# Four pieces of the modulation to a burst, in seven buffers, with half of the descriptor scratch, in a one-core hybrid decoder layer

## The chip, the cores and the metric

The kernel runs on one core of a Trainium2 chip. The metric is the device time of one execution in microseconds (us), lower is better. The kernel before took 2662.56 us (median of three runs, 2650.79 to 2666.44). Engines: PE is TensorE (matmul; PEld its weight loads), DVE VectorE, ACT ScalarE, POOL GpSimd, SP SyncE, which here issues most of the DMAs.

## The reference

One layer of a hybrid decoder on 512 prompt tokens (width 2048) and 8 sample tokens. A condition vector c gives six modulation vectors (shift, scale and gate, each for the mixer and for the FFN). One projection feeds two mixers; their outputs are concatenated, projected and added:

```python
ada = silu(c) @ w_ada + b_ada            # 2048 -> 6 * 2048
h = modulate(rmsnorm(x, g_norm_mix), shift1, scale1)
p = h @ w_in                              # 2048 -> 4896 columns
att = banded_attention(q, k, v, ...)      # window 128, ALiBi, sinks, 16 heads on 4
y, S, _ = rwkv7_mix(p[:, 1536:], ...)     # 16 heads of 64, state S (64 x 64) per head
x = x + gate1 * (concat(att, y) @ w_out)
h = modulate(rmsnorm(x, g_norm_ffn), shift2, scale2)
x = x + gate2 * (swiglu(h @ w_ffn_in) @ w_ffn_out)
y = rmsnorm(x, g_norm_final)
```

(The names of this sketch are shortened.) The RWKV-7 mixer is a recurrence over tokens, `S_t = S_{t-1} diag(w_t) + (S_{t-1} a_t) b_t^T + v_t k_t^T`. The kernel computes it in blocks of 32 tokens. Each sample token has its own old state, which is loaded, updated once and stored.

## The kernel before, in words

**Main stream.** Columns are held in two halves of 260 (256 prompt tokens and 4 sample tokens each). Every weight tile is split into a high and a low part, `wh` (ACT, L88) and `wl` (DVE, L91), of a raw tile that SP loads (L86); `mm3` (L98) makes three products of each, so one k step of a main tile is six matmuls of 260 columns. `main_tile` runs 16 k steps into a PSUM tile named `pm`. The in-projection is 39 such tiles; the out-projection's tiles are named `po` and are run in two parts of 8 k steps; `wout_part` begins the first part only when eight tiles of the concatenated heads have been loaded back from DRAM (`catl`, written earlier to `catd` by the RWKV pairs). Then comes the FFN, with sums of weight blocks in a Strassen-like scheme, some of them accumulated by POOL's DMAs.

**Side work.** Everything else is a set of generators in `self.bg`: the second part of the modulation (`ada_gen`), the RWKV pairs (8 pairs of heads: `pG` begins a pair's block matrices; a triangular solve of 31 steps on DVE, `stmp` and `Tt`, turns them into `TT`; `pu`; then the pair's recurrence over blocks, the "chain", with two small `psc` matmuls a step, ACT and DVE copying the state `Z` between them; `pY` and `pg` end the pair), the sample step (four rounds on one buffer `sS`, 512 KB loaded and stored in each), the reloading of the heads (`catl`), decode for the sample tokens and the prompt's attention (`pl` logits, `Lg`, `pt`, `pO`).

**What sets the order.** The engines run their instructions in the order in which the program issues them, so the order is fixed when the kernel is built. After each k step, `main_tile` calls `pump`, which moves a planner's clock of TensorE, `now()`, by 0.62 us and resumes each generator whose due time, `job[1]`, has come; the generator issues instructions until its next `yield`. `spent(eng, us, more)` moves an engine's planned time, and `done_at`, from which the job's next due time is taken. Work issued through `self.px` is charged so; there a `dma_start` is charged 1.0 us and 1.5 more. Since `spent` begins from the later of the engine's planned time and `done_at`, a charge to the tensor engine behind such a load moves the shared clock by the load's 2.5 us too. These are numbers of the planner, not times of the chip.

**The part around the change.** `ada_gen` makes 16 groups of 512 output columns, each from 16 pieces of weights [128 x 512] (256 KB); a piece is loaded into a tile of tag `ar` (3 buffers) and multiplied in four matmuls of 128 columns against the condition vectors, four column groups of the array. Other users of the tag are `ada_finish`, `startup`, the in-projection's spilled tiles (`sp`) and one FFN operand (`s3`). The kernel is built with the default scratch for DMA descriptors of the software queue.

Of the kernel before, what the change touches and what calls it, by code (L numbers as in the profile page):

```python
# [7 lines left out]
F32 = mybir.dt.float32  # L8
# [6 lines left out]
P = 128  # L15
KD = 16
# [47 lines left out]
class Kern:  # L64
# [190 lines left out]

    def ada_finish(self, f0, n, ps):
        nc = self.px
        res = self.w.tile([P, 512], F32, tag="ar", bufs=3, name=self.nm("adar"))
        nc.scalar.copy(res[:, :n * 128], ps[:, :n * 128])
        yield  # L260
        p2 = self.aux("adT")
        for f in range(n):
            nc.tensor.matmul(p2[:, f * 16:f * 16 + 9], res[:, f * 128:(f + 1) * 128], self.sel, start=True, stop=True)
        nc.vector.tensor_tensor(
            self.mod[:, f0:f0 + n, :],
            p2[:, :n * 16].rearrange("p (f t) -> p f t", f=n)[:, :, :9],
            self.par[:, P_BA + f0:P_BA + f0 + n].unsqueeze(2).broadcast_to([P, n, 9]),
            ALU.add,
        )
# [34 lines left out]
    def ada_gen(self):  # L304
        nc = self.px
        for c in (GT1, SH2, SC2, GT2):
            for q in range(4):
                ci = c // 4 + q
                ps = self.hold("ada")
                for k in range(KD):  # L310
                    raw = self.w.tile([P, 512], F32, tag="ar", bufs=3, name=self.nm("ar"))
                    nc.sync.dma_start(raw, self.I["w_ada2"][ci - 8, k])
                    for j in range(4):
                        self.nc.tensor.matmul(
                            ps[32 * j:32 * j + 32, 0:128], self.cT[:, k, :], raw[:, j * 128:(j + 1) * 128],
                            start=k == 0, stop=k == KD - 1, tile_position=(0, 32 * j), skip_group_check=True,
                        )
                    self.spent(self.nc.tensor, 0.3)
                    yield
                    yield  # L320
                res = self.w.tile([P, 512], F32, tag="ar", bufs=3, name=self.nm("adar"))[:, 0:128]
                nc.scalar.copy(res, ps[:, 0:128])
                yield
                p2 = self.aux("adT")
                nc.tensor.transpose(p2[:, 0:128], res, self.ident)
                nc.vector.tensor_tensor(
                    self.mod[:, 4 * ci:4 * ci + 4, :], p2[:, 0:128].rearrange("p (f t) -> p f t", f=4)[:, :, 0:9],
                    self.par[:, P_BA + 4 * ci:P_BA + 4 * ci + 4].unsqueeze(2).broadcast_to([P, 4, 9]), ALU.add)
# [41 lines left out]
    def startup(self):  # L370
        nc, I = self.nc, self.I
        xs = self.x_tiles()
        c = self.w.tile([P, 512], F32, tag="ar", bufs=3, name=self.nm("cr"))[:, 0:144]
        nc.sync.dma_start(c, I["c"].rearrange("p k t -> p (k t)"))
        k = 0
        for t, n in xs:
            nc.sync.dma_start(t, I["x"][:, k:k + n])
            k += n
        xk = [t[:, i] for t, n in xs for i in range(n)]
        nc.vector.memset(self.cT[:, :, 9:32], 0.0)  # L380
        nc.scalar.activation(self.cT[:, :, 0:9], c.rearrange("p (k t) -> p k t", t=9), AF.Silu)
        nc.scalar.activation(c[:, 0:2], self.cT[:, 0, 0:2], AF.Square)
        nc.scalar.activation(c[:, 2:4], c[:, 0:2], AF.Sqrt)
        ps = self.ps_m.tile([P, 2, 512], F32, tag="m", name="ssq1")
        for k in range(0, KD, 2):
            sq = [self.t520(t) for t in (("tC", "tD"), ("tA", "tB"))[k // 2 % 2]]
            nc.scalar.activation(sq[0], xk[k], AF.Square)
            if k % 4:
                nc.vector.tensor_tensor(sq[1], xk[k + 1], xk[k + 1], ALU.mult)
            else:  # L390
                nc.scalar.activation(sq[1], xk[k + 1], AF.Square)
            nc.vector.tensor_tensor(sq[0], sq[0], sq[1], ALU.add)
            for h in range(2):
                nc.tensor.matmul(ps[:, h, :HB], self.ones, sq[0][:, h], start=k == 0, stop=k == KD - 2)
        rstd = self.rstd_of(self.t520("tF"), ps)
        self.pcs, self.ring, self.used = {}, [], set()
        head = []
        for idx in (I_WA, I_G0, I_G1, 8, 0):
            src, m = self.w_in_src(idx)
            head.append((src, m, self.new_pc(idx)[:m, 1:513], self.SC[:m, idx]))  # L400
        self.hk = 0
        self.start(self.seq(self.h_parts(xk, rstd), self.ada_gen()))
        for k0, k1 in ((0, 2), (2, 4), (4, 8), (8, 12), (12, 14), (14, 16)):
            while self.hk < k1:
                self.pump()
            for tile_ in head:
                self.part_tile(*tile_, k0, k1)
# [44 lines left out]
    def filler(self):  # L452

        if not self.spills:
            self.pump()
            return
        idx, dram, scols = self.spills.pop(0)
        nc = self.nc
        ps = self.main_tile(self.I["w_in"][idx], self.hH, self.hL)
        t = self.w.tile([P, 512], F32, tag="ar", bufs=3, name=self.nm("sp"))  # L460
        nc.scalar.copy(t.rearrange("p (h t) -> p h t", h=2), ps[:, :, 0:256])
        nc.vector.tensor_copy(scols, ps[:, :, 256:260])
        nc.sync.dma_start(dram, t)
# [936 lines left out]
    def ffn_in(self, st):  # L1400
# [3 lines left out]
        tc, nc, I = self.tc, self.nc, self.I  # L1404
# [9 lines left out]
        sp = self.fpb.enter_context(tc.tile_pool(name="strw", bufs=1))  # L1414
# [43 lines left out]
        for ht in range(early):  # L1458
            ps = mt("pm")
# [13 lines left out]
        for i, ht in enumerate(order):  # L1473
# [7 lines left out]
            for g in range(2):  # L1481
                a11, a21 = load(ht, 0, 0, g), load(ht, 1, 0, g, places[(2 * i + g) % 4])
                a22 = load(ht, 1, 1, g, "raw")
                a12 = load(ht, 0, 1, g)
                s3 = self.w.tile([P, 512], F32, tag="ar", bufs=3, name=self.nm("s3"))
                nc.gpsimd.dma_start(a21, src(ht, 1, 1, g), accum_op=ALU.add)
                if not (old and g):
                    nc.sync.dma_start(s3, src(ht, 0, 0, g))
                    nc.gpsimd.dma_start(s3, src(ht, 1, 0, g), accum_op=ALU.add)
                if i == 0 and g == 1:  # L1490
                    for _ in norm:
                        pass
                if not old:
                    for col, a, b in ((0, a11, B11), (1, a12, B21)):
                        product(p12[:, col], weights(a), b, g)
                        if i == g == 0:
                            next(norm, None)
                            next(norm, None)
                    if g == 1:
                        first_sums(pc, p12)  # L1500
                nc.vector.tensor_tensor(a11, a21, a11, ALU.add)
                for ps, a, b in ((p45[:, 1], a21, T1), (p67[:, 0], a11, T2), (p67[:, 1], s3, T3),
                                 (p45[:, 0], a22, T4), (p3[:, 0], a12, B22)):
                    product(ps, weights(a), b, g)
                    if b is T1:
                        if old and g:
                            nc.vector.tensor_tensor(s3, a11, a22, ALU.subtract)
                        nc.vector.tensor_tensor(a12, a12, a11, ALU.add)
                        next(rest, None)
                    if i == g == 0:  # L1510
                        next(norm, None)
                        next(norm, None)
                    if g == 0:
                        continue
                    if b is T2:
                        nc.vector.tensor_tensor(pc[:, 1], p67[:, 0, :HB], pc[:, 1], ALU.subtract)  # L1516
                    elif b is T3:
                        cu = ct("cu", 2)
                        nc.vector.tensor_tensor(cu[:, 1], pc[:, 1], p67[:, 1, :HB], ALU.subtract)
                    elif b is T4:  # L1520
                        nc.vector.tensor_tensor(cu[:, 0], cu[:, 1], p45[:, 0, :HB], ALU.subtract)
                        nc.vector.tensor_tensor(pc[:, 1], p45[:, 1, :HB], pc[:, 1], ALU.add)
                        nc.vector.tensor_tensor(cu[:, 1], p45[:, 1, :HB], cu[:, 1], ALU.add)
# [217 lines left out]
```

## Time and profile before

| | us |
|---|---|
| Runs (three), median | 2662.56 (2650.79 to 2666.44) |
| Profiled execution, its own time | 2657.76 |
| Its span | 2656.0 |
| PE busy in the span | 2554.5 (96%) |
| DVE busy | 1723.8 (65%) |
| ACT busy | 1105.9 (42%) |
| POOL busy | 382.5 (14%) |
| Last matmul of the in-projection's main tiles issued at | 926.5 |
| First matmul of the out-projection at | 926.7 |
| Last matmul of the out-projection at | 1207.5 |

Busy time of PE is that of matmuls from start to modelled end; matmuls overlap, so the sum is larger than the time that they hold the array. Times of the trace are from the span's start. In rows of the trace, `x2` behind a matmul counts the records that are put together in the row; one matmul instruction of the FP32 modulation has two records. In the rows of the order below, `x4` counts instructions that are alike.

### The profile page before, as it was taken

Reading aid. Unit: us, or ns where it says so; the run is one execution under the profiler, and the core shown is the slowest. Engines: PE = TensorE matmul, PEld = TensorE weight load, DVE = VectorE, ACT = ScalarE, POOL = GpSimd, SP = SyncE. Lnnn points to the kernel's source line nnn. Section 1 sums busy time; section 2 is a strip of 40 time slices with the busy share of each in tenths; the row PEclk is TensorE's granted clock in tenths of the full one; section 3 lists DMA queues with packets and bytes.
Section 4 is the critical chain, followed back from the end, with each engine's and each line's share of the span. In section 5 each row is a group of like instructions: output and inputs, shape, how many; then the busy total and the mean of one; then the engine's idle time right before and its main releaser. Section 6 shows DMA issues by size and latency. Waiting matters only on the chain. (4 is left out here: it accounts for less than half of the span.)

```text
span 2656.0 us, 59166 instructions
## 1 busy us (share of the span) xinstructions
PE 2554.5 (96%) x23373; PEld 2340.7 (88%) x23373; DVE 1723.8 (65%) x3880; ACT 1105.9 (42%) x2153; POOL 382.5 (14%) x525
## 2 busy tenths in 40 slices
PE   7899999999999999998999999999999999999997
PEld 4677777888787889898999999999999999999997
DVE  5466767777657444678777777777777763444456
ACT  3133444545533324547544444444444532222225
POOL 0012112112112000021111212111121100000004
PEclk9999999999989999999999999999999999999999
DMA  9855445455546675245777777777777552333333
GB/s 347 294 165 154 152 126 162 149 166 160 159 153 207 203 251 146 94 160 183 191 201 204 193 208 198 191 207 198 194 208 200 155 184 92 124 125 102 116 105 106
DMA packets 241704, 460.22 MB, mean 173 GB/s; under 512 B 32353, under 2 KB 44561, under 8 KB 241393
## 3 DMA queue, kind: packets, MB, share of 16 engines
q1 hardware_dynamic: 206880, 379.88, 44.5%
q0 software_dynamic: 33904, 75.50, 13.4%
q8 instruction: 183, 3.00, 0.5%
q10 hardware_dynamic: 640, 1.05, 0.2%
q14 instruction: 97, 0.79, 0.1%
HBM read 421.73 MB, written 35.59 MB: 172 GB/s over the span
## 5 line engine op out<-in xcount | busy, mean ns | idle before, releaser
L88 ACT CAST wh<-raw 128x512 fp32r<-128x512 f32 (+2 forms) x410 | 246.9, 606 | 510.5 <-PE pf L98 278.9
L98 PE MATMUL pf<-go,wh 128*128 128x260 f32 x2560 | 414.1, 281 | 0.0
L91 DVE TENSOR_TENSOR wl<-raw,wh 128x512 fp32r<-128x512 f32 (+2 forms) x410 | 283.8, 694 | 200.4 <-ACT wh L88 194.8
L98 PEld LDWEIGHTS pf<-go,wh 128*128 128x128 f32 x2560 | 354.0, 188 | 0.1
L98 PE MATMUL pm<-hH,wh 128*128 128x260 f32 (+1 forms) x1248 | 301.3, 319 | 7.3 <-ACT wh L88 6.7
L1269 ACT CAST wh<-sr 128x512 fp32r<-128x512 f32 x320 | 198.1, 621 | 261.7 <-PE pm L1439 232.0
L1270 DVE TENSOR_TENSOR wl<-sr,wh 128x512 fp32r<-128x512 f32 x320 | 220.6, 690 | 83.0 <-ACT wh L1269 75.9
L98 PE MATMUL pm<-hH,wl 128*128 128x260 f32 (+1 forms) x1248 | 265.4, 292 | 5.2 <-DVE wl L91 5.1
L98 PE MATMUL pf<-go,wl 128*128 128x260 f32 x1280 | 267.7, 282 | 0.0
L1439 PE MATMUL pm<-xT,wh 128*128 128x260 f32 x1408 | 263.2, 286 | 4.4 <-DVE pc L1516 4.3
L98 PE MATMUL pm<-hL,wh 128*128 128x260 f32 (+1 forms) x1248 | 263.4, 291 | 0.0
L1439 PE MATMUL pm<-T,wh 128*128 128x260 f32 x1408 | 257.6, 283 | 0.0
L98 PEld LDWEIGHTS pm<-hH,wh 128*128 128x128 f32 (+1 forms) x1248 | 196.5, 191 | 57.8 <-issue 31.6
L1439 PEld LDWEIGHTS pm<-xT,wh 128*128 128x128 f32 x1408 | 216.9, 188 | 11.0 <-DVE pc L1516 6.1
L1439 PEld LDWEIGHTS pm<-T,wh 128*128 128x128 f32 x1408 | 216.9, 188 | 0.0
L98 PEld LDWEIGHTS pm<-hH,wl 128*128 128x128 f32 (+1 forms) x1248 | 197.4, 192 | 16.0 <-DVE wl L91 8.7
L1439 PE MATMUL pm<-B0H,wl 128*128 128x260 f32 x704 | 201.4, 286 | 9.6 <-DVE wl L1270 9.1
L98 PEld LDWEIGHTS pm<-hL,wh 128*128 128x128 f32 (+1 forms) x1248 | 196.9, 191 | 7.5 <-issue 5.2
L1439 PE MATMUL pm<-B0H,wh 128*128 128x260 f32 x704 | 200.3, 285 | 2.0 <-DVE acct L1206 1.7
L98 PEld LDWEIGHTS pf<-go,wl 128*128 128x128 f32 x1280 | 200.9, 188 | 0.0
L1439 PE MATMUL pm<-B0L,wh 128*128 128x260 f32 x704 | 198.9, 282 | 0.0
L1439 PE MATMUL pm<-T,wl 128*128 128x260 f32 x704 | 198.7, 282 | 0.0
(427 smaller groups left out, 5243.8 us busy)
## 6 DMA issues: line engine op xcount, KB each, us to landing
ar<-in_w_ada SPq DMA_DIRECT2D x256, 256.0 KB, 3.1
sr<-in_w_fi SPq DMA_DIRECT2D x176, 256.0 KB, 4.6
raw<-in_w_fo SPq DMA_DIRECT2D x176, 256.0 KB, 2.6
raw<-in_w_in SPq DMA_DIRECT2D x144, 256.0 KB, 3.7
araw<-in_w_ada SPq DMA_DIRECT2D x64, 512.0 KB, 6.5
raw<-in_w_fi SPq DMA_DIRECT2D x120, 256.0 KB, 4.6
s<-in_w_fi SPq DMA_DIRECT2D x80, 256.0 KB, 4.4
s<-in_w_fi POOLq DMA_DIRECT2D x80, 256.0 KB, 5.1
```

Source lines behind the costliest of these rows:

```text
L88: nc.scalar.copy(wh[:, :n], raw[:, :n])
L91: nc.vector.tensor_tensor(wl[:, :n], raw[:, :n], wh[:, :n].bitcast(F32), ALU.subtract)
L98: nc.tensor.matmul(ps[:m, bank, :HB], w, a[:, k, h, :], start=first and i == 0, stop=last and i == 2, skip_group_check=True,)
L1269: nc.scalar.copy(H, src)
L1270: nc.vector.tensor_tensor(L, src, H.bitcast(F32), ALU.subtract)
L1439: nc.tensor.matmul(ps[:, :HB], x[:, s], y, start=g == k == i == 0, stop=g == 1 and k == 3 and i == 2, skip_group_check=True)
```

## The change

The loop over 16 pieces becomes a loop over four bursts of four. A burst takes four tiles of tag `ar`, issues their four loads directly on SP (`self.nc.sync`, so that the planner isn't charged), moves its own due time by 2.5 us, yields, issues the 16 matmuls, charges the tensor engine 0.8 us, and yields twice. All users of the tag now name seven buffers. The scratch for the software queue's descriptors is set to 8192 bytes a partition, half of the default; the four more buffers take 8192 bytes a partition.

```diff
-                for k in range(KD):
-                    raw = self.w.tile([P, 512], F32, tag="ar", bufs=3, name=self.nm("ar"))
-                    nc.sync.dma_start(raw, self.I["w_ada2"][ci - 8, k])
-                    for j in range(4):
-                        self.nc.tensor.matmul(
-                            ps[32 * j:32 * j + 32, 0:128], self.cT[:, k, :], raw[:, j * 128:(j + 1) * 128],
-                            start=k == 0, stop=k == KD - 1, tile_position=(0, 32 * j), skip_group_check=True,
-                        )
-                    self.spent(self.nc.tensor, 0.3)
+                for k0 in range(0, KD, 4):
+                    raws = [self.w.tile([P, 512], F32, tag="ar", bufs=7, name=self.nm("ar")) for _ in range(4)]
+                    for k, raw in enumerate(raws, k0):
+                        self.nc.sync.dma_start(raw, self.I["w_ada2"][ci - 8, k])
+                    self.done_at += 2.5
+                    yield
+                    for k, raw in enumerate(raws, k0):
+                        for j in range(4):
+                            self.nc.tensor.matmul(
+                                ps[32 * j:32 * j + 32, 0:128], self.cT[:, k, :], raw[:, j * 128:(j + 1) * 128],
+                                start=k == 0, stop=k == KD - 1, tile_position=(0, 32 * j), skip_group_check=True,
+                            )
+                    self.spent(self.nc.tensor, 0.8)
                     yield
                     yield
...
-    nc = bacc.Bacc("TRN2", target_bir_lowering=False, num_devices=1)
+    nc = bacc.Bacc("TRN2", target_bir_lowering=False, num_devices=1, dynamic_dma_scratch_size=8192)
```

The other lines of the diff only put `bufs=7` where the tag had `bufs=3`.

How the order of the instructions changes. On TensorE, within the in-projection, a stretch with two visits to the modulation (`ada`), before:

```order
L314 MATMUL ada_7262<-ar_7469,cT 32x128 x4
L49 MATMUL psc<-Z_1732,L_803_5453 32x64 x2
L49 MATMUL pT_7482<-cst,KB_6829 128x128 x4
L98 MATMUL pm_7231<-hH,wh_7491 128x260 x2
L98 MATMUL pm_7231<-hL,wh_7491 128x260 x2
L98 MATMUL pm_7231<-hH,wl_7492 128x260 x2
L49 MATMUL psc<-Z_1732,LS_1736 64x64 x2
L98 MATMUL pm_7231<-hH,wh_7491 128x260 x2
L98 MATMUL pm_7231<-hL,wh_7491 128x260 x2
L98 MATMUL pm_7231<-hH,wl_7492 128x260 x2
L314 MATMUL ada_7262<-ar_7514,cT 32x128 x4
```

and a burst of the kernel after:

```order
L98 MATMUL pm_4010<-hH,wl_4070 128x260 x2
L49 MATMUL psc<-Z_1738,L_288_1790 32x64 x2
L98 MATMUL pm_4010<-hH,wh_4069 128x260 x2
L98 MATMUL pm_4010<-hL,wh_4069 128x260 x2
L98 MATMUL pm_4010<-hH,wl_4070 128x260 x2
L318 MATMUL ada_4052<-ar_4053,cT 32x128 x4
L318 MATMUL ada_4052<-ar_4054,cT 32x128 x4
L318 MATMUL ada_4052<-ar_4055,cT 32x128 x4
L318 MATMUL ada_4052<-ar_4056,cT 32x128 x4
L49 MATMUL psc<-Z_1738,LS_1742 64x64 x2
L98 MATMUL pm_4010<-hH,wh_4069 128x260 x2
```

The pieces stood alone between main matmuls and chain steps (`psc`); now four stand in a row. All 256 pieces stood in 261 runs of rows; they now stand in 76. The first `pG` of pairs 0 to 7 stood behind 630, 870, 1218, 1530, 1824, 2154, 2454 and 2760 of the 3744 instructions of `pm` tiles; it now stands behind 780, 1176, 1542, 2010, 2448, 2868, 3390 and 3744 (six instructions to a pump).

On TensorE, at the seam of the two projections, before:

```order
L98 MATMUL pm_11547<-hH,wh_11648 128x260 x2
L98 MATMUL pm_11547<-hL,wh_11648 128x260 x2
L98 MATMUL pm_11547<-hH,wl_11649 128x260 x2
L98 MATMUL po_11721<-cH_11377,wh_11724 128x260 x2
L98 MATMUL po_11721<-cL_11378,wh_11724 128x260 x2
L98 MATMUL po_11721<-cH_11377,wl_11725 128x260 x2
L98 MATMUL po_11721<-cH_11377,wh_11724 128x260 x2
```

and after, from the last `pm` row on:

```order
L98 MATMUL pm_10557<-hH,wl_10678 128x260 x2
L49 MATMUL pT_10753<-cst,tA_10444 128x128 x4
L49 MATMUL pG_10767<-KB_10734,tA_10444 32x64 x9
L49 MATMUL psc<-Z_1739,L_1159_7956 32x64 x2
L49 MATMUL pG_10767<-KB_10734,tA_10444 32x64 x7
L49 MATMUL pG_10768<-KB_10734,tA_10444 32x64 x5
L49 MATMUL psc<-Z_1739,LS_1744 64x64 x2
L49 MATMUL pG_10768<-KB_10734,tA_10444 32x64 x11
L49 MATMUL pu_10810<-TT,L_1350_9422 128x128 x3
L49 MATMUL psc<-Z_1739,L_1159_7956 32x64 x2
L49 MATMUL pu_10810<-TT,L_1350_9422 128x128
L49 MATMUL pY_10822<-Z_1739,RR_9140 32x64 x17
```

Behind the last `pm` row, 231 rows without a main matmul follow before the first `po` row. They hold pair 7 from `pT` and `pG` on, the end of chain 5 and chains 6 and 7, the sample step, decode, and the attention of the first two pairs of heads with part of the next.

On DVE, where the first round of the sample step (`sS`, `stt`, `sa`) stands, before:

```order
L49 TENSOR_TENSOR stt_10164<-sS_10162,X_9975 128x1024
L49 TENSOR_REDUCE L_1083_7530<-pY_10291 128x8
L49 TENSOR_REDUCE sa<-stt_10164 128x16
L49 TENSOR_SCALAR L_1083_7530<-L_1083_7530 128x8
L49 COPY Z_1733<-psc 32x64
L49 TENSOR_TENSOR stt_10164<-sa,X_9975 128x1024
L49 TENSOR_TENSOR RR_8293<-pY_10291,L_1083_7530 128x512
L49 TENSOR_TENSOR sS_10162<-sS_10162,stt_10164 128x1024
L49 TENSOR_REDUCE L_1083_7530<-RR_8293 128x8
L49 TENSOR_SCALAR Z_1733<-psc,PC_8538 64x64
L91 TENSOR_TENSOR wl_10528<-raw_10525,wh_10527 128x512
L49 TENSOR_TENSOR sS_10162<-sS_10162,stt_10164 128x1024
```

and after:

```order
L49 COPY Z_1739<-psc 32x64
L49 TENSOR_REDUCE L_1350_9422<-RR_10199 128x8
L49 TENSOR_TENSOR stt_11280<-sS_11278,X_11169 128x1024
L49 TENSOR_SCALAR Z_1739<-psc,PC_10352 64x64
L49 TENSOR_REDUCE sa<-stt_11280 128x16
L49 RECIPROCAL L_1350_9422<-L_1350_9422 128x8
L49 TENSOR_TENSOR stt_11280<-sa,X_11169 128x1024
L49 TENSOR_TENSOR RR_10199<-RR_10199,L_1350_9422 128x512
L49 TENSOR_TENSOR sS_11278<-sS_11278,stt_11280 128x1024
L49 COPY Z_1739<-psc 32x64
L49 TENSOR_SCALAR Z_1739<-psc,PC_10352 64x64
L49 TENSOR_TENSOR sS_11278<-sS_11278,stt_11280 128x1024
```

Before, the round stood between the splits `wl` of the in-projection's weights; now it stands between the copies `Z` of a chain, with no split near it. On SP the eight `catl` loads stood among the raw loads of the in- and out-projection; they now stand behind FFN weight loads (`sq`, `rstd`, `acc`) that take over buffers of decode.

More of the change, by code (lines that the diff above doesn't have):

```diff
@@ L257, in ada_finish @@
         nc = self.px
-        res = self.w.tile([P, 512], F32, tag="ar", bufs=3, name=self.nm("adar"))
+        res = self.w.tile([P, 512], F32, tag="ar", bufs=7, name=self.nm("adar"))
         nc.scalar.copy(res[:, :n * 128], ps[:, :n * 128])
@@ L309, in ada_gen @@
                 ps = self.hold("ada")
-                for k in range(KD):
-                    raw = self.w.tile([P, 512], F32, tag="ar", bufs=3, name=self.nm("ar"))
-                    nc.sync.dma_start(raw, self.I["w_ada2"][ci - 8, k])
-                    for j in range(4):
-                        self.nc.tensor.matmul(
-                            ps[32 * j:32 * j + 32, 0:128], self.cT[:, k, :], raw[:, j * 128:(j + 1) * 128],
-                            start=k == 0, stop=k == KD - 1, tile_position=(0, 32 * j), skip_group_check=True,
-                        )
-                    self.spent(self.nc.tensor, 0.3)
+                for k0 in range(0, KD, 4):
[11 more added lines that the diff above has]
+                    self.spent(self.nc.tensor, 0.8)
                     yield
                     yield
-                res = self.w.tile([P, 512], F32, tag="ar", bufs=3, name=self.nm("adar"))[:, 0:128]
+                res = self.w.tile([P, 512], F32, tag="ar", bufs=7, name=self.nm("adar"))[:, 0:128]
                 nc.scalar.copy(res, ps[:, 0:128])
@@ L372, in startup @@
         xs = self.x_tiles()
-        c = self.w.tile([P, 512], F32, tag="ar", bufs=3, name=self.nm("cr"))[:, 0:144]
+        c = self.w.tile([P, 512], F32, tag="ar", bufs=7, name=self.nm("cr"))[:, 0:144]
         nc.sync.dma_start(c, I["c"].rearrange("p k t -> p (k t)"))
@@ L459, in filler @@
         ps = self.main_tile(self.I["w_in"][idx], self.hH, self.hL)
-        t = self.w.tile([P, 512], F32, tag="ar", bufs=3, name=self.nm("sp"))
+        t = self.w.tile([P, 512], F32, tag="ar", bufs=7, name=self.nm("sp"))
         nc.scalar.copy(t.rearrange("p (h t) -> p h t", h=2), ps[:, :, 0:256])
@@ L1484, in ffn_in @@
                 a12 = load(ht, 0, 1, g)
-                s3 = self.w.tile([P, 512], F32, tag="ar", bufs=3, name=self.nm("s3"))
+                s3 = self.w.tile([P, 512], F32, tag="ar", bufs=7, name=self.nm("s3"))
                 nc.gpsimd.dma_start(a21, src(ht, 1, 1, g), accum_op=ALU.add)
```

## The prediction, made before the changed kernel was run

> **What bounds the kernel now.** I read busy time by stage first, cut at the last matmul of the in-projection's main tiles (`pm`), the last of the out-projection (`po`), and a point where the tail of the side work begins.
>
> ```profile
> 136.00:707.00 571.00, 546.72 (x6265) 442.76 (x6263) 403.65 (x1079) 261.78 (x554) 109.94 (x169) 0.98 0.51 155
> 707.00:927.00 220.00, 213.58 (x2206) 176.22 (x2207) 127.53 (x297) 78.53 (x177) 31.70 (x27) 0.96 0.59 185
> 927.00:1208.00 281.00, 268.31 (x2299) 246.98 (x2297) 166.89 (x537) 128.04 (x321) 30.26 (x51) 0.97 0.49 159
> 1208.00:2656.00 1448.00, 1415.07 (x11634) 1400.26 (x11634) 955.30 (x1793) 600.77 (x1023) 199.86 (x253) 1.00 0.61 168
> ```
>
> Columns: window, length, then busy time of PE, weight loads, DVE, ACT, POOL, granted clock, DMA share. TensorE is the bound in every stage, since the other work (RWKV pairs, their chains, the sample step, attention, modulation) is sprinkled between main matmuls. How much of a stage is main matmul, and how much modulation, the same windows by line L98 and by tile `ada` show:
>
> ```profile
> 707.00:927.00 220.00, 154.40 (x987) 129.81 (x988) 0.96 0.59 185
> 927.00:1208.00 281.00, 210.03 (x1536) 193.76 (x1534) 0.97 0.49 159
> 707.00:927.00 220.00, 29.62 (x536) 11.02 (x536) 1.33 (x5) 0.96 0.59 185
> ```
>
> Busy sums overlap, so I price by pace, from the timeline at the seam of the two projections:
>
> ```profile
> 926.25 0.41 PE L98 MATMUL pm<-hL,wh 128*128 128x260 f32 x2
> 926.50 0.40 PE L98 MATMUL pm<-hH,wl 128*128 128x260 f32 x2
> 926.73 0.40 PE L98 MATMUL po<-cH,wh 128*128 128x260 f32 x2
> ```
>
> Two matmuls per 0.24 us, 0.118 each; `po` follows `pm` without a gap. All the side work is therefore hidden by TensorE's stream, and the seam is where it would show.
>
> **The modulation's pieces.** One visit to a piece, and four pieces of twice the columns back to back in the first part of the modulation:
>
> ```profile
> 309.00 0.40 PE L98 MATMUL pm<-hH,wl 128*128 128x260 f32 x2
> 309.33 0.42 PE L314 MATMUL ada<-ar,cT 128*32 128x128 f32 x8
> 309.68 0.38 PE L98 MATMUL pm<-hH,wh 128*128 128x260 f32 x1
> 62.63 1.93 PE L273 MATMUL psc<-araw,cT 128*32 128x256 f32 x32
> ```
>
> From 309.00 to 309.68 is 0.68, less the pace of 0.24: 0.44 us for a lone visit; 256 are 114 us. Back to back a piece of 256 columns costs 1.93/4 = 0.48, so one of 128 columns 0.24. In the new order the 256 pieces stand in 76 runs: 76 × 0.44 + 180 × 0.24 = 77 us. Gain 37. Some old visits share their switch with a chain step beside them, so I take 33.
>
> Loads:
>
> ```profile
> SPq L49 <- PE ada L314: 143.9, 98, 9.3
> PE ada L314 <- DMA ar<-in_w_ada: 11.0, 12, 2.9
> ```
>
> (total wait, count, mean; between 130 and 930.) SP waits 98 times for a buffer, which costs only what TensorE then waits: 11.0 us. Four loads are now issued ahead of a yield in which the job's due time moves on by 2.5 us, so I take 10 off (between 0 and 13). SP's queue: the raw weight loads stand behind up to four `ar` loads that may wait on a buffer of the burst before; main matmuls would pay, which the end at 0 covers.
>
> **The clock by which jobs come due.** The other half is the accounting. Before, each load was charged 2.5 us and each visit 0.3 to the planner's one TensorE clock: 256 × 2.8 = 717 us by which other jobs' due times were reached sooner per main matmul. After, a burst charges 0.8: 64 × 0.8 = 51. Other jobs come due later in the main stream. In the order, the pairs' `pG` stands 51 pumps apart on average before and 71 after; pair 7's now comes after the last `pm` matmul. Where these stood in time:
>
> ```profile
> 706.12 0.86 PE L49 MATMUL pG<-KB,tA 64*32 64x64 f32 x64
> 716.34 0.20 DVE L49 TENSOR_TENSOR stmp<-Tt,As 128x31 f32<-128x31 f32 x1
> 748.34 0.18 DVE L49 TENSOR_TENSOR Tt<-Tt,stmp 128x8 f32<-128x8 f32 x1
> 888.70 0.58 PE L49 MATMUL pY<-Z,RR 128*32 128x64 f32 x19
> 899.36 1.07 PE L49 MATMUL pg<-SG,lf 128*128 128x512 f32 x4
> 903.35 0.84 SPq L1349 DMA_DIRECT2D catl<-catd  x2
> 917.73 2.58 SPq L1349 DMA_DIRECT2D catl<-catd  x2
> ```
>
> So pair 7, chains 6 and 7, the sample's four state rounds, and the loads of the concatenated heads, all under `pm` from 706 to 924 before, stand between the last `pm` and the first `po`. Decode and the first attention pairs, under `po` before, stand there too, since the out-projection starts only when the heads are loaded.
>
> When does the last `pm` end? In 707:927, 987 × 0.118 = 117 us are main matmul and 536/8 = 67 visits × 0.44 = 30 modulation. The other 73 are the side work; some 10 of them are waits or work that stay. So 927 − 63 − 33 − 10 = about 820.
>
> How long is the stretch laid bare (D)? Side work alone goes by latency. Rows:
>
> ```profile
> 738.07 0.31 PE L49 MATMUL psc<-Z,L 128*32 128x64 f32 x4
> 740.72 0.31 PE L49 MATMUL psc<-Z,L 128*32 128x64 f32 x4
> 804.41 0.33 SPq L49 DMA_DIRECT2D sS<-in_st  x1
> 826.61 0.33 SPq L49 DMA_DIRECT2D sS<-in_st  x1
> L49 DVE TENSOR_TENSOR stt<-sS,X 128x1024 f32<-128x1024 f32 x8 | 9.8, 1222 | 2.7 <-DMA sS<-in_st 2.7
> L49 DVE TENSOR_TENSOR stmp<-Tt,As 128x60 f32<-128x60 f32 (+24 forms) x31 | 8.7, 279 | 0.7
> L49 DVE TENSOR_TENSOR Tt<-Tt,stmp 128x60 f32<-128x60 f32 (+24 forms) x31 | 7.5, 243 | 0.9
> ```
>
> - From `pG` to the solve: 716.34 − 706.12 = 10, with end of chain 5: 14.
> - Solve: 31 steps of 0.28 + 0.24 = 16 us alone, 32 under `pm` (748.34 − 716.34); beside chain 6, whose 16 steps go at 2.65 (740.72 − 738.07): 16 × 2.65 = 42. I take 38.
> - Sample rounds: one buffer, loaded, updated, stored, so 22 us a round (826.61 − 804.41). Their engine work is about half of that and DMA the rest, which doesn't shrink without `pm`. The first has its load behind it and takes 9; with three more of 22: 75, chain 7 (42) inside, and 11 for what of the chain is left (4 of 16 steps).
> - Last `pY` to `pg`: 899.36 − 888.70 = 11.
> - Decode and attention's first pairs (rows below): 41.
> - Head loads: 903.35 to 917.73 and landing, 20 us; half of it beside the first `po` tiles: 10.
>
> ```profile
> 970.71 0.37 PE L49 MATMUL pl<-Kt,q 64*128 64x128 f32 x1
> 1006.73 0.88 PE L49 MATMUL pO<-PT,Vt 128*64 128x128 f32 x12
> L49 DVE CUSTOM_DVE_ANT_0 Lg<-pl,bias,der 128x256 f32<-128x256 f32 (+1 forms) x32 | 12.5, 447 | 5.1 <-PE pl L49 5.1
> ```
>
> Under `po`, first logits to first output took 36 us; the custom operation's 32 are 12.5 for four pairs. Two pairs and decode lie between 20 and 66; 41 is near the middle.
>
> D = 14 + 38 + 75 + 11 + 11 + 41 + 10 = 200. The floor is the dependent chain with nothing else: 10 + 16 + 42 + 11 + 31 + 20 = 130. The ceiling, with decode after the rounds and loads in full, 240.
>
> The out-projection stretch: 281 − 1536 × 0.118 = 100 us of it is side work; about 30 (decode and two of eight pairs) are now ahead of it, 5 of waits go with them: 246. The FFN, 1448, runs the same instructions.
>
> Sum, span: 820 + 200 + 246 + 1448 = 2714; the profiled run took 2657.76 against its span of 2656.0, so 2716. That run lies 0.2% below the median 2662.56.
>
> **Scratch.** The software queue belongs to POOL's loads, which lie in the FFN; the page's row of its issues:
>
> ```profile
> s<-in_w_fi POOLq DMA_DIRECT2D x80, 256.0 KB, 5.1
> ```
>
> Half the scratch may hold fewer such transfers at once. POOL is busy 200 of 1448 us there; if each of the 80 waited a landing, 80 × 5.1 = 408 us still fit. I cost it at 0, with 25 us above if they fall in bursts.
>
> **Two rules weighed.** The clock sags where TensorE idles:
>
> ```profile
> 28.00:36.00 8.00, 6.07 (x49) 3.71 (x49) 6.32 (x11) 2.67 (x7) 2.02 (x1) 0.79 1.03 387
> 33.07 0.64 PE L98 MATMUL pm<-hL,wh 128*128 128x260 f32 x2
> ```
>
> In a window with a granted clock of 0.79 a pair of matmuls took 0.64 instead of 0.40, 1.6 times as long. The bare stretch holds some 80 groups of 0.3 us (as at 738.07) in its dependent chain: 80 × 0.3 × 0.6 = 14 us more at that clock. Since the whole window 707:927 shows 0.96, I take 0 and keep the 14 for the range. The Trainium skill, "TensorE: Matmul & The Clock Gate", Part 1, says that the clock falls to half after an idle window of about 3.4 us; by that rule these groups would take 24 us more, and the sum would be 2740. The trace agrees as far as a clock below 1 goes; no row of it shows the clock in a stretch without main matmuls.
>
> ```profile
> 789.80 2.70 POOL L49 TENSOR_TENSOR sS<-sS,X 128x1024 f32<-128x1024 f32 x1 [29.35 <-DVE stt L49]
> 791.74 1.84 DVE L49 TENSOR_TENSOR stt<-sa,X 128x1024 f32<-128x1024 f32 x1
> ```
>
> DVE's `stt`, 1.22 on average, took 1.84 when POOL's operation began before it and ended inside it. The Trainium skill, "SBUF — State Buffer", Who interferes with whom, says that a DVE operation with two inputs in this memory is blocked by a GpSimd operation that reads it. The trace agrees here; in full it would add at most 4 × 2.7 = 11 us, within the ceiling of D.
>
> **Rivals.**
> - *Packed to its floor* (0.22): in the bare stretch all chains run beside one another. 820 + 140 + 246 + 1448 + 2 = 2656: no change. For it: main matmuls no longer stand before each chain step. Against: DVE's order puts the sample's 1.2 us operations between chain copies, one after another.
> - *Faster* (0.08): the thinner stream before 820 also loses the waits of side work, and D is near its floor. Between 130 and 930 TensorE waits 26.6 + 14.0 us for the copies of the chains:
>
> ```profile
> PEld psc L49 <- ACT Z L49: 26.6, 50, 1.9
> PE psc L49 <- ACT Z L49: 14.0, 22, 1.6
> ```
>
>  Without 35 of these the last `pm` is at 785; 785 + 140 + 246 + 1450 = 2621. It decides where D falls below about 140 with these waits gone.
> - *Slower still* (0.15): rounds behind chain 7 instead of over it, and decode behind both: D = 240 plus the low clock's 14: 2770.
> - *Ring* (0.03): 2716 + 25 = 2741.
> - That the change doesn't do what it says: the bursts are split up again (76 runs for 64 bursts says mostly not); 256 lone visits would give 2716 + 33 = 2749, inside the range.
>
> **How the numbers follow.** Forecast 2716, chance 0.52, own range 2690 to 2765. A measurement here tells 1% from no change: 2636 to 2689. Slower: 0.52 + 0.15 + 0.03 = 0.70; same 0.22; faster 0.08. For 8 in 10 I leave out the faster case and the upper half of the slowest: 2645 to 2768.
>
> **What would show it.** Last `pm` near 820; after it some 200 us with TensorE mostly idle and its granted clock down, sample rounds 20 us apart; `po` then in about 246; the rest 1448. Wrong if first `po` stands before 980 (then the gain shows), or if the FFN's stage changes length (scratch).

## The result and the profile after

The changed kernel took 2756.18 us (median of four runs, 2753.86 to 2758.62) against 2659.77 for the kernel before: a ratio of 1.037, 95% interval 1.035 to 1.039. It is slower by 96 us; 2716 was forecast, in a range from 2645 to 2768.

Busy time by stage of the changed kernel, cut at its own marks (columns as in the prediction: window, length, PE, weight loads, DVE, ACT, POOL, granted clock, DMA share). The first two rows end at the last `pm` matmul, the next four are the stretch before the first `po`, the last two the out-projection and the FFN:

```profile
136.00:707.00 571.00, 542.10 (x6508) 475.96 (x6508) 337.41 (x899) 223.61 (x471) 82.07 (x130) 0.97 0.59 188
707.00:839.00 132.00, 127.14 (x1242) 111.47 (x1241) 92.92 (x238) 61.43 (x133) 24.92 (x40) 1.00 0.27 81
839.00:857.00 18.00, 14.73 (x240) 11.28 (x239) 9.63 (x30) 10.05 (x22) 6.71 (x10) 0.91 0.85 274
857.00:895.00 38.00, 26.55 (x172) 21.09 (x170) 23.98 (x111) 12.27 (x31) 5.50 (x6) 0.55 0.61 188
895.00:983.00 88.00, 36.91 (x380) 23.93 (x379) 58.27 (x104) 21.14 (x63) 29.06 (x25) 0.56 0.35 103
983.00:1070.50 87.50, 63.98 (x401) 45.84 (x400) 28.51 (x115) 23.46 (x77) 6.17 (x9) 0.54 0.26 80
1070.50:1313.20 242.70, 235.67 (x1866) 218.58 (x1866) 143.66 (x423) 108.27 (x251) 18.73 (x33) 0.98 0.37 121
1313.20:2756.70 1443.50, 1415.63 (x11636) 1401.64 (x11635) 955.41 (x1793) 601.35 (x1023) 197.26 (x248) 1.00 0.59 167
```

The dense stream has a hole. Between 839 and 1070 TensorE's rows are busy for 142 of 231 us, from 857 on no engine is near full, and TensorE's granted clock there is 0.54 to 0.56. The out-projection is shorter than before (243 us against 281), the FFN is the same length (1443.5 against 1448).

The timeline of TensorE at the edges of the hole, as at the seam of the kernel before:

```profile
838.83 0.40 PE L98 MATMUL pm<-hH,wl 128*128 128x260 f32 x2
839.07 0.60 PE L49 MATMUL pT<-cst,tA 128*128 128x128 f32 x4
980.73 2.05 PE L49 MATMUL pg<-SG,lf 128*128 128x512 f32 x4
1070.45 0.99 PE L98 MATMUL po<-cH,wh 128*128 128x260 f32 x3 [1.14 <-ACT cH L143]
```

The last `pm` is at 839, the last pair's `pg` at 981, the first `po` at 1070. So the hole is 142 us of pairs, chains and sample step, and 90 us of decode, attention and head loads. Each such place in time comes from one profiled execution; the runs of one kernel lie up to 23 us apart (2651 to 2674 for the kernel before), so a few us between two seams decide nothing.

And a burst in the stream (x32 are the 16 matmuls of four pieces):

```profile
304.44 1.08 PE L318 MATMUL ada<-ar,cT 128*32 128x128 f32 x32
```

Four pieces take 1.08 us together, where four lone visits were priced at 4 × 0.44 = 1.76.

### The profile page after: what moved, and what is told of

It reads as the page before. It is cut to its first block, busy times and chain, and to the rows that moved or that the text cites. A ratio compares the mean times of both kernels' runs of the same rounds, so it can differ in the third digit from the quotient of the medians.

```text
span 2756.7 us, 59171 instructions
## 1 busy us (share of the span) xinstructions
PE 2573.5 (93%) x23373; PEld 2383.9 (86%) x23373; DVE 1719.0 (62%) x3880; ACT 1097.4 (40%) x2147; POOL 381.2 (14%) x525
## 5 line engine op out<-in xcount | busy, mean ns | idle before, releaser
L98 PE MATMUL pm<-hH,wh 128*128 128x260 f32 (+1 forms) x1248 | 289.5, 312 | 7.4 <-ACT wh L88 6.6
```

The lines of the kernel that those rows point to most:

```text
L98: nc.tensor.matmul(ps[:m, bank, :HB], w, a[:, k, h, :], start=first and i == 0, stop=last and i == 2, skip_group_check=True,)
```

## The experiments

**e1: the bursts, with the planner's clock moved on.**

```diff
-                    self.spent(self.nc.tensor, 0.8)
-                    yield
-                    yield
+                    for _ in range(4):
+                        self.spent(self.nc.tensor, 2.0)
+                        yield
```

> The changed kernel with its bursts, seven buffers and half scratch, but each burst is followed by four charges of 2.0 us to the planner's TensorE clock, one at each resume, instead of one of 0.8. In its order no row stands between the last pm and the first po, and the pairs begin where they did in the kernel before. Theory A (the whole loss comes from the planner's clock, which moves less, so that side work is laid bare; bursts by themselves gain): no bare stretch, and about 2660 - 33 - 10 = 2617 us. Theory B (the bursts, the seven buffers or the smaller scratch hurt by themselves): 2660 us or more. Between them, theory C (the bursts gain only about half of what was forecast, as the holding time of the pieces in the two traces hints, 98.5 to 80.7 us): 2630 to 2645 us.

Measured: 2651.43 us, ratio 0.9955 (0.9942 to 0.9969) to the kernel before. The hole is gone (last `pm` at 911.2, first `po` at 911.4), and with it 105 us; theory A holds for the loss. The gain of the bursts lies in none of the three expected ranges, though: 13 us by the medians, where 43 (A), 15 to 30 (C) or none (B) were expected, counted from 2660.

**e2: the accounting alone, without bursts.** In the kernel before:

```diff
-                    nc.sync.dma_start(raw, self.I["w_ada2"][ci - 8, k])
+                    self.nc.sync.dma_start(raw, self.I["w_ada2"][ci - 8, k])
...
-                    self.spent(self.nc.tensor, 0.3)
+                    self.spent(self.nc.tensor, 0.2)
```

> The kernel before with lone pieces, three buffers and full scratch; only the loads of the modulation's second part no longer charge the planner, and a piece charges 0.2 instead of 0.3 us. Theory A: pairs come late (pair 7's pG behind the last pm) and a stretch of about 200 us is laid bare, with none of the bursts' gain: 2740 to 2790 us. Theory B: 2660 us, since nothing that it blames is there.

Measured: 2744.16 us, ratio 1.0299 (1.0282 to 1.0315). Its timeline:

```profile
861.11 0.41 PE L98 MATMUL pm<-hH,wl 128*128 128x260 f32 x2
861.71 0.66 PE L49 MATMUL pT<-cst,tA 128*128 128x128 f32 x4
1018.43 0.80 PE L98 MATMUL po<-cH,wh 128*128 128x260 f32 x2
```

A hole of 157 us and a loss of 80, with three buffers, the full scratch and lone pieces. So the planner's clock alone makes the loss, and e1 says that the rest of the change by itself makes none. Here the work that stood bare as pairs, chains and sample step took 140 us, as in the changed kernel, but decode doesn't stand ahead of the first `po`: from the last `pg` it takes 17 us instead of 90, and the out-projection 280 instead of 243.

**e3: the buffers and the scratch alone.** In the kernel before:

```diff
-... tag="ar", bufs=3, ...
+... tag="ar", bufs=7, ...
-    nc = bacc.Bacc("TRN2", target_bir_lowering=False, num_devices=1)
+    nc = bacc.Bacc("TRN2", target_bir_lowering=False, num_devices=1, dynamic_dma_scratch_size=8192)
```

> The kernel before with seven buffers and half scratch, lone pieces and the old charges. Theory A: 2645 to 2662 us, the waits of TensorE for pieces (11 us before) partly gone, the FFN's stage 1448 us as before. Theory B, if buffers or scratch are at fault: slower than 2680 us, in the FFN's stage if it is the scratch.

Measured: 2659.22 us, ratio 0.9979 (0.9961 to 0.9997). The smaller scratch costs nothing that can be seen: the FFN, from the last `po` on, took 1446 us against 1448 before. The buffers do what they were priced at in the in-projection. Waits of TensorE (total, count, longest; between 130 and 930):

```profile
PE ada L314 <- DMA ar<-in_w_ada: 1.8, 5, 0.6
PE psc L49 <- ACT Z L49: 9.8, 14, 2.1
```

Those for pieces fell from 11.0 us to 1.8, and the last `pm` came at 916 instead of 927. By the medians about half of these 10 us are given back later (below, on the clock).

**e5 and e6: what lone pieces and bursts cost where they stand.** In e3's and in e1's program only the first piece of each group is multiplied, so they leave out 240 of the 256 pieces and don't compute the modulation; here e3's:

```diff
-                    for j in range(4):
+                    for j in range(4 if k == 0 else 0):
...
-                            start=k == 0, stop=k == KD - 1, tile_position=(0, 32 * j), skip_group_check=True,
+                            start=True, stop=True, tile_position=(0, 32 * j), skip_group_check=True,
```

> The kernel before with seven buffers and half scratch (as e3), all loads and charges kept, but of the 16 pieces of each group only the first is multiplied (16 pieces of 256; the modulation's second part is so not computed). What the 240 lone visits cost where they stand. Theory P (a visit costs 0.44 us wherever it stands): the last pm at 916 - 106 = 810, the total some 100 us below 2659. Theory C (a visit beside a chain step shares its switch and covers the wait for the chain's copies, so that part of it comes back as waits of psc): the last pm at 835 to 855, and waits of psc for ACT's copies above 30 us instead of 9.8.

> The same cut on e1's program (bursts, four charges of 2.0): only the first piece of each group is multiplied. What the bursts cost where they stand. Theory P: 72 us by the forecast's prices (77 less the 16 pieces left), the last pm at about 840. Theory C: bursts cover few of the chain's waits, so their full price comes back too: about 65 to 75 us, the last pm at 836 to 846, close to where e5 ends; the waits of psc stay near 36 us.

Measured: e5 2603.73 us (0.9776, 0.9744 to 0.9808), e6 2623.50 (0.9855, 0.9812 to 0.9897). The seam of e3, of e5, of e1 and of e6:

```profile
916.21 0.40 PE L98 MATMUL pm<-hH,wl 128*128 128x260 f32 x2
```
```profile
846.47 0.40 PE L98 MATMUL pm<-hH,wl 128*128 128x260 f32 x2
```
```profile
911.16 0.40 PE L98 MATMUL pm<-hH,wl 128*128 128x260 f32 x2
```
```profile
866.89 0.40 PE L98 MATMUL pm<-hH,wl 128*128 128x260 f32 x2
```

The 240 lone pieces cost 916 − 846 = 70 us, 0.29 each and not 0.44; in bursts they cost 911 − 867 = 44 us, 0.18 each. So bursts save 26 us of their own, against the 33 of the forecast. The whole kernel's medians say the same of the difference, though not of each price: the lone pieces cost 2659 − 2604 = 55 us there, the bursts 2651 − 2624 = 28.

e5 ended where theory C had put it (835 to 855). Of its reason one half holds. The waits of `psc` didn't rise, they were 10.3 us; but other waits came in place of the pieces. These three were 5.2, 1.1 and 0.9 in e3, and are in e5

```profile
PE pA L49 <- DVE L L49: 9.3, 2, 6.8
PE pm L98 <- DVE wl L91: 6.8, 4, 2.6
PE pt L49 <- DVE RR L49: 6.1, 4, 2.4
```

In all, TensorE's waits between 130 and the last `pm` rose from 21 us to 38 in e5, and from 48 to 54 in e6. So 17 of the 106 − 70 = 36 us between price and cost stand as waits in e5 instead. More of what makes a lone visit cheaper stands in the matmuls' starts. In each of the two kernels I took every stretch between two `pm` matmuls that holds only the named work (in the last row a visit to `ada` and then chain steps), and its length less the 0.118 of the pace (worked out from the trace, median us and number of stretches):

```
                     before         after
ada alone            0.45 (110)     1.10 (35)    one piece / a burst
psc alone            0.36 (108)     0.36 (115)
ada and psc          0.71 (62)      1.34 (22)
```

Beside a chain step a lone piece costs 0.71 − 0.36 = 0.35; that the two share one turn away from the main matmuls is my reading. Alone it is the 0.45 that was priced, and a burst alone is 1.10, so 0.217 for each further piece. With 110 visits at 0.45 and the other 146 at 0.35 the mean is 0.39, and with the waits added e5 gives (70 + 17)/240 = 0.36; the two nearly meet.

The two ends differ, though: without the pieces e6 still ends its in-projection at 867, 20 us behind e5, where 836 to 846 was expected. The order that e1's charges make is worse by that for the rest of the work, and this is where most of the 26 went. Why it is worse was looked for in e1's waits of TensorE:

```profile
PE psc L49 <- ACT Z L49: 36.4, 26, 5.5
```

36.4 us instead of e3's 9.8. My reading was that the planner's clock jumps by 2.0 at four turns in a row, so that chain steps come due at each of them, sooner than ACT has copied the state. The next runs don't bear it out.

**e8: larger charges.** e1 with 2.8 for 2.0.

```diff
-                        self.spent(self.nc.tensor, 2.0)
+                        self.spent(self.nc.tensor, 2.8)
```

> e1 with charges of 2.8 us instead of 2.0: a burst then moves the planner by 11.2 us, as four pieces did before; pairs come a little sooner (pair 7's pG behind 2538 instead of 2694 pm matmuls). Theory A with a saturation (once the stretch is covered, more charge only makes chain steps follow each other more closely and wait): within 6 us of e1's 2651. If the covered tail still binds: faster than 2640.

Measured: 2654.78 us, ratio 0.9963 (0.9945 to 0.9981); the same as e1. Once the tail is covered, more charge buys nothing. The jumps are larger here than in e1, yet the waits are less in sum, and the last `pm` is at 918:

```profile
PE psc L49 <- ACT Z L49: 21.4, 32, 3.5
```

**e9 and e10: an even clock, and bursts spread out.** e9 is the changed kernel with the main tiles' `pump` alone changed; e10 adds the second edit:

```diff
-            self.pump()
+            self.pump(1.2)
...
-                    self.done_at += 2.5
+                    self.done_at += 8
```

> The changed kernel with one number changed: the main tiles of the in-projection move the planner's clock by 1.2 us a k step instead of 0.62; the bursts charge 0.8 as in the changed kernel. The clock so moves evenly instead of in jumps behind each burst. In its order no row stands between the last pm and the first po, and pair 7's pG stands behind 2735 pm matmuls. Theory A (the loss is the planner's clock): no bare stretch, at or below e1's 2651. Theory D (the bursts' own 25 us, by e5 and e6, are eaten by charges that come in jumps: chain steps then follow one another at every k step and wait for their copies, 36.4 us in e1 against 9.8 in e3): with an even clock these waits fall below 20 us, the last pm comes before 900, and the total is 2625 to 2645. If D is wrong: last pm near 911, total 2645 to 2660.

> e9 with a burst's due time moved on by 8 us instead of 2.5, so that bursts are spread over most of the in-projection (the last behind 3240 pm matmuls instead of 2082). If it matters that bursts and chains share the stream evenly, 3 to 10 us below e9; if not, within 4 us of it.

Measured: e9 2646.04 us, ratio 0.9937 (0.9918 to 0.9956); e10 2635.80 us, 0.9892 (0.9857 to 0.9927). One number in the planner turns the loss of 96 us into a gain of 18, and two into one of 29. Waits of `psc` and last `pm` in e9, then the same and the seam in e10:

```profile
PE psc L49 <- ACT Z L49: 17.7, 23, 2.7
909.24 0.40 PE L98 MATMUL pm<-hH,wl 128*128 128x260 f32 x2
```
```profile
PE psc L49 <- ACT Z L49: 22.4, 28, 2.8
896.20 0.40 PE L98 MATMUL pm<-hH,wl 128*128 128x260 f32 x2
896.44 0.40 PE L98 MATMUL po<-cH,wh 128*128 128x260 f32 x2
```

Theory A holds again: no hole, and faster than e1. Theory D fails: e9's waits fell below 20 as it said, 19 us less than in e1, but its last `pm` at 909 came only 2 us sooner and its total of 2646 lies in the range for D being wrong. In e10 the waits are more than in e9 and the last `pm` is at 896. So these waits are not what held the in-projection back. What helps is the bursts spread over the in-projection instead of crowded into its first part: 10 us in the total, at the upper end of the 3 to 10 expected. Why, and what else cost e1 its 20 us, stays open. e10 is the fastest complete version of this study.

**e12: lone pieces under the even clock.** In e3's program:

```diff
-            self.pump()
+            self.pump(1.2)
...
-                    nc.sync.dma_start(raw, self.I["w_ada2"][ci - 8, k])
+                    self.nc.sync.dma_start(raw, self.I["w_ada2"][ci - 8, k])
...
-                    self.spent(self.nc.tensor, 0.3)
+                    self.spent(self.nc.tensor, 0.2)
+                    self.done_at += 1
```

> The kernel before with seven buffers and half scratch (as e3), lone pieces, and the even clock of e9 and e10: the loads charge nothing, a piece charges 0.2 us and moves its own due time by 1.0, the main tiles of the in-projection move the planner by 1.2 us a k step. Pairs begin about where they do in e10 (pair 7's pG behind 2550 instead of 2658 pm matmuls), the pieces stand in 258 runs. If the bursts are what makes e10 faster (e5 and e6: 70 us for lone pieces, 44 for bursts): the last pm at 915 to 930 and 2655 to 2668 us. If it is the even clock: the last pm near 896 and 2635 to 2645 us.

Measured: 2677.63 us, ratio 1.0053 (1.0036 to 1.0071), the last `pm` at 940:

```profile
940.00 0.40 PE L98 MATMUL pm<-hH,wl 128*128 128x260 f32 x2
```

That is outside both ranges (2655 to 2668 if the bursts make e10 fast, 2635 to 2645 if the even clock does). The even clock by itself doesn't make e10 fast; with lone pieces it is slower than the kernel before. The step from e12 to e10 is 2677.63 − 2635.80 = 42 us in the total and 940 − 896 = 44 in the in-projection. That is more than the 26 between e5 and e6, and 24 us of it are that e12 ends later than e3 (916). So e12 to e10 is no clean price of the bursts. Why lone pieces do worse under the even clock than under the old charges was not tried and stays open; 154 of e12's visits stand alone, at 0.45, against 108 in e3, but at 0.10 more for each that is some 5 us of the 24.

**e4 and e11: is the hole long because the clock is low?** The changed kernel with extra matmuls that nobody reads, at each turn of the loops behind the last `pm`: three (e4) or one (e11).

```diff
+    def keep(self, ps):
+        for _ in range(3):
+            self.nc.tensor.matmul(ps[:, 0, 0:128], self.ident, self.cst[:, 0:128], start=True, stop=True, skip_group_check=True)
+        self.pump()
...
-                        self.pump()
+                        self.keep(pd)
...
+                    while self.bg:
+                        self.keep(pd)
                 self.drain()
```

> The changed kernel with three small matmuls more (128 columns, into a bank that nobody reads) at each turn of the loops that wait for the pairs and the sample step after the last pm: 723 in all, nothing else. The stretch from the last pm (839) to the last pg (981) has a granted clock of 0.55. If that clock binds it, the clock rises above 0.8 there and the stretch of 142 us shrinks by 15 to 35 us, the time with it. If the stretch goes by the latency of DVE, ACT and DMA, it stays within 5 us or grows by up to 30 us.

> e4 with one small extra matmul a turn instead of three, 241 in all. In e4 the clock was 0.98 in the bare stretch but the extra matmuls, 80 us of them, stood in the chains' way (last pg 1035 against 981). With a third of them: if the low clock binds, the last pg comes before 975; if not, 981 to 1000.

Measured: e4 2789.98 us, e11 2715.62 (one run each). The stages of e11, cut at its last `pm`, last `pg`, first and last `po`:

```profile
835.00:973.20 138.20, 119.06 (x1262) 100.05 (x1260) 91.52 (x242) 42.53 (x115) 38.34 (x38) 0.90 0.47 139
973.20:990.80 17.60, 8.66 (x31) 5.48 (x29) 3.69 (x13) 3.43 (x6) 4.75 (x7) 0.50 0.80 282
990.80:1270.50 279.70, 270.72 (x2244) 248.11 (x2243) 166.26 (x522) 128.70 (x322) 20.72 (x36) 0.96 0.38 120
```

With the clock at 0.90 instead of 0.60 (its mean from 839 to 983 in the changed kernel) the chains' part took 138 us instead of 142, extra matmuls included. The last `pg` at 973 falls into the range expected for a clock that binds (before 975), but only because the last `pm` came 4 us sooner, at 835. In e4, at 0.98, the stretch took 198 us (837 to 1035), and another 33 us of extra matmuls stood ahead of its first `po` at 1068.5. So e11's 4 us are what the clock gave less what 241 extra matmuls cost, and no run tells the two apart: what the low clock costs the chains stays open.

What made e11 41 us faster than the changed kernel was not asked for. Its extra rows changed the order that the builder chose behind them, and decode and most of the attention's start now stand behind the first `po`. From `pg` to the first `po` it takes 18 us instead of 90, and the out-projection, which hides that work, 280 instead of 243: by these stages a net of 35 us that the changed kernel loses by their place. e2's stages, 17 and 280, agree.

**e7: the head stores and loads on ACT's queue.**

```diff
-        nc.sync.dma_start(self.catd[hp], yc)
+        nc.scalar.dma_start(self.catd[hp], yc)
...
-            nc.sync.dma_start(t, self.catd[k])
+            nc.scalar.dma_start(t, self.catd[k])
```

> The changed kernel with the stores and loads of the concatenated heads (catd, catl) issued by ACT instead of SP, nothing else. In the changed kernel pair 7's store stands on SP behind an FFN weight load that waits for decode's buffers, and was issued at 1062, 76 us after its data. If that queue holds up the first po, it comes from 1070 to 1010 to 1045 and the time falls by 10 to 40 us. If TensorE's own order does (227 rows of chains, decode and attention stand before the first po there too), the first po stays within 8 us of 1070 and the time within 10 us of 2756.

Measured: 2750.22 us (one run), first `po` at 1060, last `pg` at 975, 85 us apart instead of 90. Pair 7's store now stands on ACT:

```profile
1044.54 0.33 ACTq L49 DMA_DIRECT2D catd<-V  x1
```

It was still issued 70 us late, behind the attention's work in ACT's order, and the first `po` at 1060 lies between the two expectations (1010 to 1045, and within 8 of 1070); that it is 10 us sooner than in the changed kernel comes with a last `pm` at 828 instead of 839. So this run doesn't tell SP's queue from TensorE's order. The changed kernel's own trace says more: TensorE's rows ahead of the first `po` run to 1069, and it then waits 1.14 us for its head (the row shown above), so sooner loads alone could win little there. e2 and e11 show that the order decides.

## Why the prediction was right, and where its sizes were off

The direction and the mechanism were right: the likeliest case was that the planner's clock moves too little, that pair 7, chains 6 and 7, the sample rounds and the attention's start stand bare, and that this costs more than the bursts gain. e1 and e9 (no hole, 105 and 110 us less) and e2 (the hole without bursts) show it. The size was 56 us (2716 against the 2659.8 measured here), the measured one 96. By its own steps, on the span:

| Step | Forecast | Measured |
|---|---|---|
| last `pm` | 820 | 839 |
| pairs, chains, sample rounds (14 + 38 + 75 + 11 + 11) | 149 | 142 |
| decode, attention, head loads (41 + 10) | 51 | 90 |
| out-projection | 246 | 243 |
| FFN | 1448 | 1443.5 |
| span | 2714 | 2756.7 |

- **Decode and attention, mis-sized: 51, and 90 measured.** I took 41 as near the middle between 20 and 66, whose working the prediction doesn't show; it names the custom operation's time and the pace under `po`. TensorE's own time in a stretch without main matmuls was left out. Its rows for the logits, of the kernel before (960 to 1052) and after (983 to 1070):

```profile
L49 PE MATMUL pl<-Kt,q 64*128 64x256 f32 (+1 forms) x32 | 8.5, 379 | 0.0
```
```profile
L49 PE MATMUL pl<-Kt,q 64*128 64x256 f32 (+1 forms) x24 | 11.1, 617 | 4.5 <-DMA q<-qd 3.0 <-DVE sm L49 0.9 <-ACT PT L49 0.6
```

 The first row is the logits of four pairs of heads, so the 24 of the second are those of three, where the forecast counted two. 379 ns became 617 at a clock of 0.54, and TensorE was busy for 64 of the 87.5 us. The price of the low clock, 14, was taken as 0 because the window 707:927 showed 0.96, which is no row for a stretch without main matmuls. I had put it on the chains, where its size stays open (e11). In decode and attention the logits alone (these 24 and as many of `Ks`) are 48 × 0.238 = 11 us longer by their means, an estimate; no run here raised the clock in that part alone. The forecast's reason for this work standing bare, that the out-projection starts only when the heads are loaded, doesn't hold either: it needs them in e2 and e11 too, and decode stands behind the first `po` there.
- **Last `pm`, 19 late.** The bursts' own gain is 26 by e5 and e6 instead of 33. The waits for pieces fell, but not to 0:

```profile
PE ada L318 <- DMA ar<-in_w_ada: 4.9, 6, 3.4
```

 4.9 of 11.0 are left, 6 us of the 10 gained. So 11 of the 19 have a place; the other 8 stay open.
- **Chains and sample rounds, right within 7.** The solve took 39.5 us (855.2 to 894.7) where 38 was forecast. The rounds came 18 to 20 us apart: POOL's operation began at 896.11, 914.31, 932.53 and 952.26, against 22 in the sum.

```profile
896.11 2.34 POOL L49 TENSOR_TENSOR sS<-sS,X 128x1024 f32<-128x1024 f32 x1 [0.47 <-DVE stt L49]
952.26 2.34 POOL L49 TENSOR_TENSOR sS<-sS,X 128x1024 f32<-128x1024 f32 x1 [9.39 <-DVE stt L49]
L49 DVE TENSOR_TENSOR stt<-sa,X 128x1024 f32<-128x1024 f32 x4 | 7.6, 1903 | 0.1
```

- **The two rules weighed.** The clock's: the stretch without main matmuls ran at 0.54 to 0.60. The Trainium skill, "TensorE: Matmul & The Clock Gate", Part 1, says that the clock falls to half after an idle window of about 3.4 us. The trace agrees with the half, but not with the condition: from 857 to 895 the clock was 0.55, and TensorE's longest idle time there was 2.73 us (before 871.27). By that rule the sum would have been 2740, nearer than mine, though its 24 us stood on the chains, and it was decode and attention that ran over. The blocked memory port's: DVE's `stt` on `sa` took 1.77 to 2.04 us in all four rounds, each time with POOL's operation under way; in the kernel before it took 1.84 and 1.80 in the two rounds where POOL's operation overlapped it and 1.225 in the two where it didn't. This agrees with the Trainium skill, "SBUF — State Buffer", Who interferes with whom; at 4 × 0.7 = 3 us it is small, and the chain's length held.
- **Rivals.** *Packed to its floor*: the hole is 231 us, not 140. *Faster*: the waits of `psc` for ACT were 17.6 us after, 14.0 before; they didn't go. *Slower still* named a hole of 240 and the low clock, 2770, and came nearer in its number than my sum, but by another cause: the rounds lay over chain 7 as in my sum, and it was decode and attention that were long. *Ring*: the FFN kept its length, and e3 shows no cost of the scratch. *The bursts split up*: its 2749 is the nearest number of all, by luck, since the bursts stood in 76 runs and took 1.08 us each.
- **What was to show it.** Last `pm` near 820, `po` in about 246 and the FFN unchanged were so within 3%; sample rounds near 20 us and the lower clock too. That TensorE would be mostly idle in the hole was not so: its rows are busy for 142 of the 231 us.

## What to carry to other kernels

Where a planner with an internal clock decides what is hidden, every charge is also a pace for all other jobs: an edit that makes one job cheaper on paper can leave the others behind, so compare where the last of them stands against the end of the stream that covers them. When a burst replaces lone visits, price the visit where it stands (here 0.29 us and not 0.44, because part of it came back as waits when the pieces were left out, and many visits stood beside other small work), and give the clock back to the other jobs: one constant turned 3.7% slower into 0.6% faster, and spreading the bursts made it 1.1%. Work that is laid bare should be priced with its own matmuls in the sum, at the clock that such a stretch shows (0.54 to 0.60 here).

## What the runs showed of the hardware that was not expected

The granted clock fell while TensorE's rows were without a gap. In e1, whose in-projection ended 15 us before that of the kernel before, two windows of the out-projection:

```profile
1010.00:1020.00 10.00, 10.00 (x123) 9.00 (x122) 3.32 (x13) 4.58 (x17) 0.00 (x0) 0.90 0.16 53
1020.00:1030.00 10.00, 10.00 (x76) 9.60 (x76) 0.82 (x2) 0.00 (x0) 0.00 (x0) 0.50 0.09 27
L49 PE MATMUL psc<-PTs,sq 128*64 128x2 f32 x32 | 4.1, 249 | 0.0
L98 PE MATMUL po<-cH,wh 128*128 128x260 f32 x9 | 3.3, 460 | 0.0
```

TensorE is busy for 10.00 of 10 us and has a clock of 0.50. What it runs there (the last two rows, 1018 to 1034) is decode: matmuls that move two columns, each behind a load of new weights, between a few main matmuls, which then take 460 ns, where those of the FFN take 281 in the kernel before. In the kernel before the same place had 0.77 at its lowest:

```profile
1030.00:1040.00 10.00, 10.00 (x104) 9.36 (x100) 1.58 (x7) 1.10 (x2) 0.00 (x0) 0.77 0.14 50
```

A lowered clock shows in two such windows of 10 us in the kernel before and in three in e1 and in e3, so it differs from version to version. What e1 and e3 had gained by the seam was gone behind it: their last `po` came at 1207 and 1211, against 1207.5 before. Their out-projections ran at a clock of 0.94 and took 296 and 295 us, against 0.97 and 281; 0.03 of 296 is 9 us, so by this estimate the clock is the larger part. Why the episodes are longer there was not tried.

The second surprise is of the builder, not of the chip: rows added in front of a place (e11) changed which work it put ahead of the first `po`. The order is thus not only the program's, as the description of the kernel has it; independent work is moved when the kernel is built. The source says so too: `wout_part` follows `attn_phase` at once, with the loads of the heads already issued, so decode stands ahead of the first `po` in the built kernel and not in the program.
